# Three of the four lo parts of each MLP pair of a hybrid diffusion step: an accumulating DMA in place of a GpSimd subtraction

## The chip, the cores and the metric

The kernel runs on one core of a Trainium2 chip. The metric is the time of one execution in device microseconds (us), as the median of several executions. Five engines work side by side, each through its own instructions in order: TensorE (PE, matmuls; PEld is its weight load), VectorE (DVE), ScalarE (ACT), GpSimd (POOL) and SyncE (SP, which here only issues DMAs). An instruction waits at the head of its engine's queue until the semaphores that it needs have been raised, and everything behind it on that engine waits with it.

## What is computed

One layer of a diffusion backbone over 128 context and 1024 latent tokens: a token mixer (differential attention and a convolution branch), then a gated MLP with a depthwise convolution of width 3. The part that matters here is the first half of the MLP (`D_MODEL` = 1024, `D_FF` = 2816):

```python
h = rmsnorm(x, lp['w_norm2']) * (1.0 + scale2) + shift2
up = dwconv(h @ lp['w_up'], lp['w_ffn_dw'])
ff = (jax.nn.silu(up[..., :D_FF]) * up[..., D_FF:]) @ lp['w_down']
x = x + gate2 * ff
```

## The kernel before

All weights and activations are float32. A matmul is made of three: every operand is split into a hi part, which is the value rounded to the type float32r, and a lo part, which is the value less its hi part, and the product is hi·hi + hi·lo + lo·hi. So each block of weights needs two tiles, `whi` and `wlo`, ahead of its first use. `prep_to` makes them, in the order of the list `SEQ`: a cast on ACT writes `whi` (L180), and a subtraction `raw - whi` writes `wlo` (L182), on DVE for the first two blocks and on POOL for all others.

The tokens stand in three groups of 384 columns. `w_up` is worked through in 22 pairs of blocks of 128 columns (one of the left half, one of the right half of `up`). Pair 0 is done plainly. Pairs 1 to 21 (`pair(i)`) treat the first two token groups with seven products instead of eight (sums of quarters of the weights against sums of quarters of the activations), and the third group plainly. For this each pair needs four operand sets of 128 x 1024, `w{i}_0` to `w{i}_3`, called w0 to w3 here: w0 and w3 lie in buffers of the tag `raw`, w1 and w2 in buffers of the tag `rawx`, two buffers of each. `fetch_pair` loads them with three DMAs on SP: L155 (all of w3's buffer, 512 KB), L156 (half of w0's) and L157 (half of w2's), 256 KB each; the other halves are sums that DVE makes (L164), called just ahead of the cast in `prep_to`. A buffer is loaded again once the cast and the subtraction that read it are done.

One pair is 11 units of 12 matmuls (L1487): seven products (`prod`) and four quarters of the third token group (`third`). Each set is used in two products and one or two of those quarters. Its successor is prepared inside the same pair: w0 after the products that use it (`prep(5)` behind `p6`), w1 behind `p7`, w2 behind `c2`, w3 at the end. `whi` and `wlo` have one buffer for each place in the ring of four, so a cast waits until PE's last matmul with that set is done.

PE writes into PSUM banks named `f`, `T`, `O` and `S`; ACT (L1566, L1596, L1603) and DVE (L1563) take the results out and free the banks. The depthwise convolution of a pair's two halves follows on ACT (L1477, the first tap; L1618, silu) and DVE (L1479, taps two and three, two for each half; L1620, the product of the halves), and SP stores the result to `scr_fscr` (L1538). In the first pairs DVE also works off a list of small dot products in the background (L1194). After the pairs comes the second half of the MLP (`down`), where POOL already issues accumulating DMAs of 384 KB (L1683, tile `hx`).

The order of the instructions on each engine isn't written out: the program's scheduler sets it from its own timeline, when the kernel is built.

Of the kernel before, what the change touches and what calls it, by code (L numbers as in the profile page):

```python
# [8 lines left out]
F32 = mybir.dt.float32  # L9
F32R = mybir.dt.float32r  # L10
AF = mybir.ActivationFunctionType
ALU = mybir.AluOpType
# [86 lines left out]
SEQ = ORDER + FILL + TAIL + MERGE + WO + WO + FFN  # L99
# [10 lines left out]
class Kernel:  # L110
# [59 lines left out]
    def prep_to(self, p):  # L170
        nc = self.nc
        while self.prepped < min(p, len(SEQ)):
            self.fetch_to(self.prepped + 1)
            raw, make = self.raw.pop(0)
            pool = next(self.wring)
            hi, lo = (pool.tile([128, 1024], F32R, tag=t, name=t, bufs=3 if pool is self.wp else 1)
                      for t in ("whi", "wlo"))
            if make:
                make()
            nc.scalar.copy(hi, raw)  # L180
            eng = nc.vector if self.prepped < 2 else nc.gpsimd
            eng.tensor_tensor(out=lo, in0=raw, in1=hi.bitcast(F32), op=ALU.subtract)  # L182
            self.w[self.prepped] = (SEQ[self.prepped], hi, lo)
            self.prepped += 1
        self.fetch_to(self.prepped + self.fetch_ahead)

    def take(self, name, ahead=2):
        p = self.pos
        assert SEQ[p] == name, (SEQ[p], name)
        self.prep_to(p + 1)  # L190
        self.pos += 1
        got = self.w.pop(p)
        self.late_prep = p + 1 + ahead
        return got[1], got[2]
# [1713 lines left out]
```

## Time and profile before

| what | us |
|---|---|
| median of 3 runs | 1810.08 (1808.92 to 1811.53) |
| the profiled execution, whole | 1811.61 |
| the profiled execution, span from first to last instruction | 1809.8 |
| PE busy | 1690.3 (93% of the span) |
| DVE busy | 1253.8 (69%) |
| ACT busy | 691.0 (38%) |
| POOL busy | 819.0 (45%), of which the two groups of L182: 325.7 and 107.2 |

Busy time is summed over the span. PE is the engine with the least idle time, but the table doesn't tell what ends its waits in one stage. For that the views by stretch and by wait are needed. The stretch of the program in which the change works is about 1040 to 1500 us from the span's start.

### The profile page before, as it was taken

Reading aid. Unit: us, or ns where it says so; the run is one execution under the profiler, and the core shown is the slowest. Engines: PE = TensorE matmul, PEld = TensorE weight load, DVE = VectorE, ACT = ScalarE, POOL = GpSimd, SP = SyncE. Lnnn points to the kernel's source line nnn. Section 1 sums busy time; section 2 is a strip of 40 time slices with the busy share of each in tenths; the row PEclk is TensorE's granted clock in tenths of the full one; section 3 lists DMA queues with packets and bytes.
Section 4 is the critical chain, followed back from the end, with each engine's and each line's share of the span. In section 5 each row is a group of like instructions: output and inputs, shape, how many; then the busy total and the mean of one; then the engine's idle time right before and its main releaser. Section 6 shows DMA issues by size and latency. Waiting matters only on the chain.

```text
span 1809.8 us, 25328 instructions
## 1 busy us (share of the span) xinstructions
PE 1690.3 (93%) x9928; PEld 1649.2 (91%) x9928; DVE 1253.8 (69%) x1594; ACT 691.0 (38%) x1106; POOL 819.0 (45%) x507
## 2 busy tenths in 40 slices
PE   5999889989989999899998999999999999999997
PEld 3889889988989999888998999899999999999997
DVE  5868994698796663697679787878677675333335
ACT  4424454445544553311226533333334336211111
POOL 2545782683873422544343443534434447533311
PEclk8999999999999999999999999999999999999999
DMA  8264223424325424665842222222222226623102
GB/s 307 89 187 142 95 83 100 143 74 136 100 77 177 153 85 134 233 226 179 289 160 85 84 80 70 89 69 80 85 79 73 73 81 194 186 99 99 62 13 105
DMA packets 102446, 220.49 MB, mean 122 GB/s; under 512 B 10004, under 2 KB 60856, under 8 KB 100280
## 3 DMA queue, kind: packets, MB, share of 16 engines
q1 hardware_dynamic: 45264, 120.15, 19.6%
q10 hardware_dynamic: 51592, 79.08, 13.8%
q0 software_dynamic: 5472, 19.66, 3.7%
q8 instruction: 78, 1.28, 0.3%
q14 instruction: 40, 0.33, 0.1%
HBM read 161.55 MB, written 57.30 MB: 121 GB/s over the span
## 4 chain that ended last, share of the span: by engine, by line
PE 45%; DVE 22%; issue 9%; DMA 5%; ACT 4%; POOL 4%; ACTq 0%; POOLq 0%; SPq 0%; DVEq 0%
PE f L230 14%; PE T L230 7%; DVE conv L639 5%; PE S L1487 5%; PE T L1487 4%; PE f L1487 4%; PE O L230 3%; PE O L1487 2%; DVE X L1479 2%; DVE mx L781 2%; DMA tg<-scr_gscr 2%; PE O L822 2%; DVE S L1194 2%; DVE e L794 2%; POOL wlo L182 1%
## 5 line engine op out<-in xcount | busy, mean ns | idle before, releaser
L182 POOL TENSOR_TENSOR wlo<-raw,whi 128x1024 fp32r<-128x1024 f32 x124 | 325.7, 2627 | 468.8 <-ACT whi L180 445.6
L230 PE MATMUL f<-h1h,whi 128*128 128x384 f32 x680 | 233.7, 346 | 4.1 <-ACT gt L602 3.3
L230 PE MATMUL f<-h1l,whi 128*128 128x384 f32 x680 | 234.6, 345 | 0.0
L230 PE MATMUL f<-h1h,wlo 128*128 128x384 f32 x680 | 232.3, 342 | 0.0
L180 ACT CAST whi<-raw 128x1024 fp32r<-128x1024 f32 x126 | 131.9, 1047 | 233.8 <-PE f L230 49.4
L1479 DVE SCALAR_TENSOR_TENSOR X<-X,vec,X 128x1153 f32<-128x1153 f32 x88 | 159.1, 1812 | 75.8 <-ACT X L1477 75.2
L639 DVE SCALAR_TENSOR_TENSOR conv<-glu,vec,conv 128x967 f32<-128x967 f32 x120 | 199.3, 1661 | 1.1
L182 POOL TENSOR_TENSOR wlo<-rawx,whi 128x1024 fp32r<-128x1024 f32 x42 | 107.2, 2558 | 104.7 <-ACT whi L180 97.4
L652 POOL TENSOR_TENSOR conv<-conv,tap 128x200 f32<-128x200 f32 x120 | 115.3, 961 | 68.5 <-ACT tap L646 66.0
L230 PEld LDWEIGHTS f<-h1h,whi 128*128 128x128 f32 x680 | 130.3, 192 | 5.8 <-ACT gt L602 4.0
L230 PEld LDWEIGHTS f<-h1l,whi 128*128 128x128 f32 x680 | 130.9, 192 | 0.4
L230 PEld LDWEIGHTS f<-h1h,wlo 128*128 128x128 f32 x680 | 130.2, 192 | 0.2
L781 DVE TENSOR_REDUCE mx<-S 128x1 f32<-128x1152 f32 (+1 forms) x72 | 88.7, 1231 | 32.0 <-PE S L775 32.0
L783 ACT ACTIVATE e<-S,mx 128x1152 f32<-128x1152 f32 (+1 forms) x72 | 81.2, 1128 | 68.4 <-DVE mx L781 57.0
L646 ACT ACTIVATE tap<-glu,vec 128x200 f32<-128x200 f32 x120 | 55.5, 462 | 106.6 <-POOL conv L652 90.6
L230 PE MATMUL T<-ff,whi 128*128 128x384 f32 x360 | 92.2, 335 | 1.5 <-ACT hx L1679 1.5
L230 PE MATMUL f<-ff,whi 128*128 128x384 f32 x340 | 87.1, 335 | 0.6 <-ACT hx L1679 0.6
L180 ACT CAST whi<-rawx 128x1024 fp32r<-128x1024 f32 x42 | 43.8, 1049 | 110.0 <-DVE rawx L164 74.2
L774 PE MATMUL S<-K,q 128*128 128x384 f32 (+1 forms) x200 | 69.3, 347 | 13.4 <-ACT e L783 13.4
L811 DVE TENSOR_TENSOR atl<-T,ath 128x512 fp32r<-128x512 f32 (+1 forms) x100 | 52.0, 538 | 31.5 <-ACT ath L810 31.2
L1239 DVE SCALAR_TENSOR_TENSOR hx<-f,g,hx 128x128 f32<-128x128 f32 (+1 forms) x64 | 31.6, 515 | 58.8 <-PE f L230 58.7
L1239 DVE SCALAR_TENSOR_TENSOR hx<-T,g,hx 128x256 f32<-128x256 f32 (+1 forms) x66 | 32.4, 512 | 54.3 <-PE T L230 54.0
(435 smaller groups left out, 4947.1 us busy)
## 6 DMA issues: line engine op xcount, KB each, us to landing
raw<-in_wst SPq DMA_DIRECT2D x105, 512.0 KB, 4.0
X<-scr_fscr POOLq DMA_DIRECT2D x20, 576.0 KB, 5.0
scr_fscr<-X SPq DMA_DIRECT2D x22, 512.0 KB, 3.0
scr_gscr<-gate ACTq DMA_DIRECT2D x48, 192.0 KB, 2.0
tg<-scr_gscr SPq DMA_DIRECT2D x24, 384.0 KB, 4.2
ada<-in_ada SPq DMA_DIRECT2D x8, 1024.0 KB, 9.8
araw<-in_ada ACTq DMA_DIRECT2D x16, 512.0 KB, 4.1
K<-scr_kscr ACTq DMA_DIRECT2D x4, 1920.0 KB, 8.2
```

Source lines behind the costliest of these rows:

```text
L180: nc.scalar.copy(hi, raw)
L182: eng.tensor_tensor(out=lo, in0=raw, in1=hi.bitcast(F32), op=ALU.subtract)
L230: nc.tensor.matmul(out, lhsT=a, rhs=b, start=(i == 0), stop=(i == n - 1))
L639: t = nc.vector.scalar_tensor_tensor(out=o, in0=glu[:, j:j + CSPLIT], scalar=w[:, j:j + 1], in1=o, op0=ALU.mult, op1=ALU.add)
L646: nc.scalar.activation(out=p, in_=glu[:, CSPLIT + j:CONVW + j], func=AF.Copy, scale=w[:, j:j + 1])
L652: t = nc.gpsimd.tensor_tensor(out=o, in0=o, in1=p, op=ALU.add)
L774: nc.tensor.matmul(S[:, j, :cw], lhsT=qt[:, c, o:o + 128], rhs=self.K[:, c, ks], start=True, stop=False)
L781: nc.vector.tensor_reduce(out=mx[:, 1:2], in_=src, axis=AX.XY, op=ALU.min)
L783: nc.scalar.activation(out=e[:, :w].rearrange("p (a b) -> p a b", a=nk), in_=src, func=AF.Exp, scale=-1.0, bias=mx[:, 1:2], accum_out=self ...
L1239: nc.vector.scalar_tensor_tensor(out=d, in0=ps[:, o:o + ln], scalar=gate[:, j, c:c + 1], in1=d, op0=ALU.mult, op1=ALU.add)
L1479: nc.vector.scalar_tensor_tensor(out=y[:, :L], in0=u[:, t:t + L], scalar=w[:, t:t + 1], in1=y[:, :L], op0=ALU.mult, op1=ALU.add)
L1487: nc.tensor.matmul(ps[:, :CH], lhsT=a[:, ws], rhs=b[:, k], start=first and k == 0 and i == 0, stop=last and k == 3 and i == 2)
```

## The change

For the sets w0, w1 and w2 of pairs 2 to 21 (60 of the 84 sets) the subtraction on POOL goes. In its place ACT writes minus the hi part into `wlo` (a copy with scale -1, behind the cast), and a DMA on POOL's queue adds the raw values to it, from one place in SBUF to another. Set w3 of every pair, and all of pair 1, keep the subtraction.

```diff
             nc.scalar.copy(hi, raw)
-            eng = nc.vector if self.prepped < 2 else nc.gpsimd
-            eng.tensor_tensor(out=lo, in0=raw, in1=hi.bitcast(F32), op=ALU.subtract)
+            if self.by_dma(SEQ[self.prepped]):
+
+                nc.scalar.activation(out=lo, in_=hi.bitcast(F32), func=AF.Copy, scale=-1.0)
+                nc.gpsimd.dma_start(out=lo.bitcast(F32), in_=raw, accum_op=ALU.add)
+            else:
+                eng = nc.vector if self.prepped < 2 else nc.gpsimd
+                eng.tensor_tensor(out=lo, in0=raw, in1=hi.bitcast(F32), op=ALU.subtract)
...
+    def by_dma(self, name):
+
+        if name[0] != "w" or name[1] == "o":
+            return False
+        i, u = map(int, name[1:].split("_"))
+        return i > 1 and u < 3
```

Lines below this place move down by 12 (L1487 is L1499 after the change); L182 becomes L187 where it stays, the negating copy is L183 and the DMA L184.

The scheduler orders the other engines anew. Three places show it. The first is ACT at the preparation of pair 5's sets; `whi_9817`, `whi_9852` and `whi_9890` are w0, w1 and w2 of pair 5. Before:

```order
L1566 COPY acc_9759<-S_6703 128x384
L1477 ACTIVATE X1_9148<-X0_9141,vec_67 128x1153
L180 CAST whi_9817<-raw_9753 128x1024
L180 CAST whi_9852<-rawx_9755 128x1024
L180 CAST whi_9890<-rawx_9754 128x1024
L1596 COPY X0_9141<-S_6703 128x384
L1477 ACTIVATE X1_9148<-X0_9141,vec_67 128x1153
```

The same place after the change, where `whi_9826`, `whi_9862` and `whi_9901` are those sets:

```order
L1578 COPY acc_9768<-S_6703 128x384
L1189 DMA X2_9366<-in_ada2 128x1024
L180 CAST whi_9826<-raw_9762 128x1024
L183 ACTIVATE wlo_9827<-whi_9826 128x1024
L180 CAST whi_9862<-rawx_9764 128x1024
L183 ACTIVATE wlo_9863<-whi_9862 128x1024
L180 CAST whi_9901<-rawx_9763 128x1024
L1608 COPY X0_9141<-S_6703 128x384
L183 ACTIVATE wlo_9902<-whi_9901 128x1024
L1489 ACTIVATE X1_9148<-X0_9141,vec_67 128x1153
```

Each cast has a negating copy behind it, and the copy for w2 stands ahead of the next first tap (L1477, now L1489).

The second place is POOL at the same sets, before:

```order
L182 TENSOR_TENSOR wlo_9818<-raw_9753,whi_9817 128x1024
L182 TENSOR_TENSOR wlo_9853<-rawx_9755,whi_9852 128x1024
L182 TENSOR_TENSOR wlo_9891<-rawx_9754,whi_9890 128x1024
L182 TENSOR_TENSOR wlo_9940<-raw_9752,whi_9939 128x1024
L182 TENSOR_TENSOR wlo_10012<-raw_9944,whi_10011 128x1024
```

POOL there after the change:

```order
L184 DMA wlo_9827<-raw_9762 128x1024
L184 DMA wlo_9863<-rawx_9764 128x1024
L184 DMA wlo_9902<-rawx_9763 128x1024
L187 TENSOR_TENSOR wlo_9952<-raw_9761,whi_9951 128x1024
L184 DMA wlo_10024<-raw_9956 128x1024
```

Three of four subtractions are DMA issues now, and the one for w3 stays in its place.

The third place is PE where pair 5 begins; `whi_9817` and `wlo_9818` are w0 of pair 5, the first row is the last matmul with a set of pair 4 ahead of it. Before:

```order
L1487 MATMUL S_6703<-h2h_8906,wlo_9698 128x384
L1487 MATMUL f_9953<-hx_8657,whi_9817 128x384 x2
L1487 MATMUL f_9953<-hx_8657,wlo_9818 128x384
L1487 MATMUL f_9953<-hx_8657,whi_9817 128x384 x2
L1487 MATMUL f_9953<-hx_8657,wlo_9818 128x384
```

PE there after the change, where `whi_9826` and `wlo_9827` are w0 of pair 5 and `whi_9862` is w1:

```order
L1499 MATMUL S_6703<-h2h_8906,wlo_9706 128x384
L1499 MATMUL f_9965<-hx_8657,whi_9826 128x384 x2
L1499 MATMUL T_9979<-h2h_8906,whi_9826 128x384
L1499 MATMUL T_9979<-h2l_8907,whi_9826 128x384
L1499 MATMUL O_9992<-hx_8658,whi_9826 128x384 x2
L1499 MATMUL f_10007<-hx_8659,whi_9862 128x384 x2
L1499 MATMUL T_10029<-op_8660,whi_9862 128x384 x2
L1499 MATMUL f_9965<-hx_8657,wlo_9827 128x384
```

Ten matmuls with hi parts, from five chains, now stand ahead of the first one with the lo part, where there were two. Between the last matmul with w0 of pair 4 and this one stand 51 matmuls; before, 50.

## Rows read from the trace of the kernel before

**Rows 1.** Windows: busy time by engine, 1040 to 1500 us (engine, busy us, instructions).
```profile
1040.00:1500.00 460.00, 443.19 (x2511) 440.70 (x2511) 350.36 (x407) 170.80 (x193) 201.46 (x77) 0.99 0.24 79
```
**Rows 2.** Waits of PE, 1040 to 1500 us (us in total, times, longest).
```profile
PE S L1487 <- DVE acc L1563: 6.6, 3, 2.9
PE S L1487 <- DVE X L1563: 5.5, 2, 3.0
PE f L1487 <- DVE X L1563: 3.2, 1, 3.2
PE f L1487 <- POOL wlo L182: 1.0, 1, 1.0
```
**Rows 3.** One line's or tile's instructions, 1055 to 1500 us (ns minimum/median/maximum).
```profile
L1479 DVE SCALAR_TENSOR_TENSOR X<-X,vec,X x76: 1408/1422/3575, 1055.6 to 1497.0; 128x1153 f32<-128x1153 f32 x76
...
L164 DVE TENSOR_TENSOR raw<-raw x18: 677/680/2887, 1066.9 to 1471.5; 128x512 f32<-128x512 f32 x18
```
**Rows 4.** Timeline of DVE ahead of PE's wait at 1143.9 (start us, us).
```profile
1136.70 2.85 DVE L164 TENSOR_TENSOR raw<-raw 128x512 f32<-128x512 f32 x1
...
1140.81 3.50 DVE L164 TENSOR_TENSOR rawx<-raw 128x512 f32<-128x512 f32 x2
...
1146.16 0.54 DVE L1563 TENSOR_TENSOR acc<-S,acc 128x384 f32<-128x384 f32 x1
```
**Rows 5.** Timeline of POOL beside it.
```profile
1135.52 3.49 POOL L182 TENSOR_TENSOR wlo<-rawx,whi 128x1024 fp32r<-128x1024 f32 x1
1140.77 2.39 POOL L182 TENSOR_TENSOR wlo<-raw,whi 128x1024 fp32r<-128x1024 f32 x1 [1.76 <-ACT whi L180]
```
**Rows 6.** Timeline of DVE and POOL ahead of PE's wait at 1219.
```profile
1216.42 3.54 DVE L1620 TENSOR_TENSOR X<-X 128x1153 f32<-128x1153 f32 x1
...
1215.88 2.87 POOL L182 TENSOR_TENSOR wlo<-raw,whi 128x1024 fp32r<-128x1024 f32 x1 [3.74 <-ACT whi L180]
```
**Rows 7.** Windows of PE with the granted clock (busy us, matmuls, clock).
```profile
1054.50:1057.90 3.40, 3.40 (x13) 0.51 0.69 253
```
**Rows 8.** Chain that ended last: a run of matmuls without a gap.
```profile
711.71 8.33 PE T L230 x48
```
**Rows 9.** Timeline of DVE and POOL, 1529.5 to 1533 us, where POOL issues DMAs.
```profile
1529.60 1.41 DVE L1479 SCALAR_TENSOR_TENSOR X<-X,vec,X 128x1153 f32<-128x1153 f32 x1
1531.11 1.36 DVE L1620 TENSOR_TENSOR X<-X 128x1153 f32<-128x1153 f32 x1
...
1530.51 1.77 POOL L1683 DMA_DIRECT2D hx<-scr_xscr  x2
```
**Rows 10.** Lines by form, ACT, 1040 to 1500 us (busy us, mean ns, idle before).
```profile
L1477 ACT ACTIVATE X<-X,vec 128x1153 f32<-128x1153 f32 x39 | 49.0, 1261 | 7.2 <-DMA scr_fscr<-X 4.5 <-DVE X L1563 2.1
L180 ACT CAST whi<-raw 128x1024 fp32r<-128x1024 f32 x39 | 40.9, 1049 | 99.7 <-PE S L1487 39.4 <-DMA raw<-in_wst 31.9 <-DVE raw L164 16.8
```
**Rows 11.** Waits of DVE, 1040 to 1500 us.
```profile
DVE X L1479 <- ACT X L1477: 62.5, 29, 5.6
```
**Rows 12.** Tile hx, 1510 to 1640 us: the accumulating DMAs of 384 KB.
```profile
L1683 POOL DMA_DIRECT2D hx<-scr_xscr x12: 848/1232/1866, 1521.0 to 1545.8; - x12
...
DMA to landing us min/median/max: 5.8/9.2/16.6
```
**Rows 13.** DMA queues, 1555.5 to 1557.8 us: accumulating packets alone (packets, MB, share).
```profile
q0 software_dynamic: 176, 0.49, 109.8%
```
**Rows 14.** DMA issues of the page (KB each, median us to landing).
```profile
X<-scr_fscr POOLq DMA_DIRECT2D x20, 576.0 KB, 5.0
```
**Rows 15.** Timeline of ACT: the cast of w0 of pair 5.
```profile
1091.44 1.06 ACT L180 CAST whi<-raw 128x1024 fp32r<-128x1024 f32 x1 [4.25 <-PE S L1487]
```
**Rows 16.** Waits of the DMA queue of SP, 1040 to 1500 us.
```profile
SPq L156 <- POOL wlo L182: 188.6, 18, 18.0
...
SPq L157 <- POOL wlo L182: 48.6, 18, 4.1
```

## The prediction, made before the changed kernel ran

> **What bounds the kernel now.** I read the busy times of the stretch first, then what PE waits for there, then what the engine it waits for was doing. The change lies between 1040 and 1500 us. There PE is busy for 443 of 460 us and runs at 0.99 of its clock, so at most some 17 us of idle time and a little clock can be won; POOL is busy for only 201 us, so its own load isn't the limit [rows 1]. Nearly all of PE's idle time is six waits for DVE, to free a PSUM bank: 6.6 + 5.5 + 3.2 = 15.3 us. One wait of 1.0 us is for a `wlo` from POOL [rows 2]. DVE, at 350 of 460 us, isn't full either; it comes late at six places.
>
> Why it comes late is seen by setting the two timelines side by side. The first of L164's additions takes 0.68 us at its median and up to 2.89, the tap of L1479 1.42 and up to 3.58: two kinds of run, not a spread [rows 3]. At 1136.70 the addition starts 1.2 us after a POOL subtraction of 3.49 us has begun and ends just after it; at 1140.81 two more take 3.50 us beside the next subtraction [rows 4, 5]. So a DVE instruction that reads two SBUF tensors stands still while POOL subtracts. In that row of work DVE lost 2.85 - 0.68 = 2.2 us and 3.50 - 2 x 0.68 = 2.1 us, and the bank was read out at 1146.16, when PE had stood for 2.9 us [rows 2, 4]. Ahead of the wait at 1219, L1620 takes 3.54 us beside a subtraction [rows 6], against 1.36 us without one [rows 9], again 2.2 us lost. The other four waits show one or the other picture.
>
> **What the change removes.** 60 of the 77 subtractions in this stretch go, some 60 x 2.6 us of POOL time that nobody waits for, and with them the hold on DVE. The question is whether the DMA issue that takes their place holds DVE as well. Where POOL issued accumulating DMAs for 1.77 us without a pause, L1479 took 1.41 us and L1620 1.36 us, their undisturbed times [rows 9]. So I take the issue as free for DVE; the other end, that it holds DVE for its own 0.85 to 1.87 us [rows 12], is a rival below. What comes back at the six waits: the two of the L1620 picture (5.5 us together) get 2.2 us each, since the subtraction for w3 a little earlier stays: 4.4 us. The other four (6.6 + 3.2 = 9.8 us) have two holds of 2.1 or 2.2 us ahead of them, more than each wait is long, so I take all: 9.8 us. Sum 14.2 us.
>
> PE's clock adds to it. After four of these waits PE shows 3.4 us at the lower level, 0.5 of 2.4 GHz: 13 matmuls in the 3.4 us [rows 7], some of them counted at the edges, where the undisturbed step of 8.33 / 48 = 0.174 us [rows 8] would give 19.6. At half the clock a stretch of 3.4 us loses at most 1.7 us, and 6.6 x 0.174 = 1.1 us by the count; I take 1.4 x 4 = 5.6 us, gone with the waits. The gain is 14.2 + 5.6, about 20 us.
>
> **What it adds on ACT.** 60 negating copies of 128 x 1024. L1477 takes 1.26 us for 1153 columns, the cast 1.05 us for 1024 [rows 10], so 1.05 to 1.12 us each, 67 us at most. ACT has the room, 171 of 460 us [rows 1]. Those who stand behind a copy in ACT's queue are the first tap L1477, for which DVE already waits 62.5 us in 29 waits [rows 11], and the copies out of PSUM, for which PE waits. The order shows the copy for w2 ahead of the next first tap. A delay of 1.1 us hits PE only where DVE is then late for a bank again: nothing at the low end, 1.1 us at each of the six places at the high end, 6.6 us. I take half, 3 us, because the DVE work ahead of these places is 2 to 4 us shorter than now.
>
> **What it adds as latency.** A lo part was ready 2.4 to 3.5 us after its cast [rows 5]. Now it is the copy, the issue and the landing. No row shows a transfer of 512 KB from SBUF onto SBUF. The nearest are the accumulating DMAs of 384 KB: 5.8 us at the least, which is the one that found the queue nearly empty, 9.2 at the median and 16.6 at the most, where up to six stood in the queue [rows 12]. Size: in a stretch that holds only such packets, 176 packets (18 of them of 4 bytes) fill 16 engines for 2.3 us, so 16 x 2.3 x 1.098 / 158 = 0.256 us for one of 3072 bytes, or 0.34 us for 4096 [rows 13]; with 8 packets on each engine (128 rows over 16) 512 KB take 8 x (0.34 - 0.256) = 0.7 us longer. A plain load of 576 KB on the same queue lands in 5.0 us [rows 14]. So the low end is 5.0, the high end 16.6; I take 5.8 + 0.7 = 6.5, near the low end, since between 1040 and 1500 us the DMA engines are busy for 0.24 of the time [rows 1].
>
> The tightest place is w0 of pairs 5, 9, 12, 16 and 19. Its cast starts when PE has done the last matmul with the old w0 [rows 15], and in the new order 51 matmuls stand between that one and the first that reads the new lo part: 51 x 0.174 = 8.9 us. Needed are 1.05 + 1.1 + 6.5 = 8.65, and some 0.2 us of hand-over: 8.85 us. It just fits, with nothing to spare. w2 in pairs 6, 13 and 20 has 61 to 63 matmuls (10.6 to 10.9 us), with two more ACT instructions ahead of its copy, and just fits as well. w0 of pairs 8 and 15 has 62; all others have 69 or more, 12 us. So every microsecond that the landing takes beyond 6.5 costs up to 8 us. At 5.8 nothing is lost; I take 0.3 us on average, 2 us.
>
> The Trainium skill (DMA: Bandwidth & Descriptors, Anatomy of one DMA — SWDGE (gpsimd) path) gives 2.0 us and the bytes over 436 GB/s for a DMA from POOL, by which 512 KB would take 3.2 us, and these 2 us would be nought; the trace speaks against it for this kind, with 5.8 us for 384 KB at the least [rows 12].
>
> Last, the loads. A buffer is free only when the DMA that reads it has landed, some 6 us later than now. SP waits at L157 for w1's lo part, 48.6 us in 18 waits (2.7 us each), and the issue of L156 stands behind it, which itself waits 188.6 us in 18 waits (10.5 us each) for the subtraction of w3 [rows 16]. That stays, and covers the 6 us on average: nothing.
>
> Sum: 1809.8 - 20 + 3 + 2 = 1794.8 us of span. The profiled execution took 1811.6 us with a span of 1809.8, and lay 1.5 above the median of 1810.1; so the median should be 0.3 us above the span, **1795 us**.
>
> **Rivals.** First, the ACT copies give half of it back: the delays come to 6.6 us and two of the six waits stay with their clock (5 us more): 1795 + 3.6 + 5 = 1804 us. For it speaks that DVE already waits for L1477; against it that DVE's lost time is larger than the copies.
>
> Second, the lo parts land late, the one that ends on the other side. With 9 us the eight tight places lose 8 x 2.5 = 20 us less the 2 counted, 1813 us, and this is the point from which it decides. With 10 us they lose 28, the two places with 62 matmuls join with 2 x 1.5, and five lower-clock stretches add 7: 1795 - 2 + 38 = 1831 us. For it speak the median of 9.2 us and that some transfers share the queue with the loads, or that w1's and w2's casts follow closely; against it that the 9.2 belongs to a full queue.
>
> A second way to be late is at the start: that POOL can't write a DMA's descriptors while DVE runs. If each issue had to wait out one L1479, 1.4 us [rows 3], the eight places would lose 8 x 1.4 = 11 us more, 1806 us. Against it: the issues beside L1479 and L1620 stayed at 0.9 us each [rows 9], and these two lines are the bulk of DVE's work in the stretch. The Trainium skill (SBUF — State Buffer, SBUF: two separate sides) has it as a rule that DVE in a mode that uses both its ports keeps GpSimd from writing descriptors; no row here shows a DVE instruction that does so.
>
> Third, the change doesn't do what it says for DVE: the issue holds it for 1.2 us in place of 2.1. Then 0.9 of each 2.1 us comes back, 20 x 0.43 = 9 us, less 5: 1806 us. Rows 9 speak against it.
>
> **How the numbers follow.** The forecast has 0.52, the ACT rival 0.18, the late landing 0.18 (0.06 near 9 us, which ends as no change, 0.12 beyond), the late start 0.04, the hold by the issue 0.08. A run of this kernel can tell about 0.2%, 3.6 us, from no change. The last two end at the bound of 1806 and count half as faster, half as the same. Faster: 0.52 + 0.16 + 0.02 + 0.04 = 0.74; same: 0.02 + 0.06 + 0.02 + 0.04 = 0.14; slower: 0.12. The range reaches from 1788 us (all of the 20 us, nothing added, 1790, and some small waits more) to 1814 us, the point at which the late landing decides; 0.12 lie above and some 0.07 below.
>
> **What would show it.** Right: L1479, L1620 and L164 at their short times in nearly every run but beside w3's subtraction; PE's waits for DVE between 1040 and 1500 us at 3 us or less in place of 15; the accumulating DMAs landing in 6 to 7 us, and no waits of PE for a DMA into `wlo`. Wrong: PE waiting for that DMA at the beginning of pairs 5, 9, 12, 16 and 19, or DVE's long runs still there.

## The result, and the profile after

The changed kernel takes **1790.28 us** (median of 4 runs, 1788.7 to 1791.63), beside 1810.8 us for the kernel before on the same chip: a ratio of 0.9886 (0.9873 to 0.9898). The forecast was 1795 us, the range 1788 to 1814 us. The profiled execution has a span of 1788.3 us in place of 1809.8.

Where the 21.5 us of span went can be told from three points of the trace. The first matmul of the 22 pairs starts at 965.6 us in place of 968.4; that is ahead of the change's place, and over all the kernels of this study this point lies between 964.0 and 969.6 us (once, where the stage ahead was edited, at 980.9), so it isn't the change's. From that matmul to the last of the pairs, 2916 of them, it takes 532.7 us in place of 551.3: 18.7 us less. What follows takes 290.0 us in place of 290.2. This middle part is called the pair stage below.

Busy time by engine, 1040 to 1500 us of the kernel after (PE, PEld, DVE, ACT, POOL, each with its instructions; granted clock, DMA share, GB/s), which answers to [rows 1]:

```profile
1040.00:1500.00 460.00, 454.55 (x2604) 452.46 (x2603) 291.96 (x416) 237.72 (x265) 113.55 (x85) 1.00 0.61 152
```

PE is busy for 11 us more, DVE for 58 us less with the same work and more of it done, ACT for 67 us more, POOL for 88 us less, and the DMA share is 0.61 in place of 0.24. Waits of PE in the same stretch, all that are listed (us in total, times, longest), for [rows 2]:

```profile
PE S L1499 <- DVE X L1575: 3.3, 1, 3.3
PE O L1499 <- DMA wlo<-raw: 0.7, 1, 0.7
PE S L1499 <- DVE acc L1575: 0.6, 1, 0.6
PE S L1499 <- DMA wlo<-rawx: 0.5, 1, 0.5
PE S L1499 <- ACT X L1608: 0.3, 1, 0.3
```

The six waits for DVE, 15.3 us, have become two of 3.9 us. A seventh of 0.5 us, which [rows 2] don't show, is gone, and so is the wait for POOL; 1.2 us of waits for the new DMAs have come. The instructions of single lines on DVE, 1055 to 1500 us (ns minimum/median/maximum), for [rows 3]:

```profile
L1491 DVE SCALAR_TENSOR_TENSOR X<-X,vec,X x75: 1408/1422/3039, 1057.6 to 1498.5; 128x1153 f32<-128x1153 f32 x75
...
L164 DVE TENSOR_TENSOR raw<-raw x18: 677/680/694, 1059.5 to 1451.8; 128x512 f32<-128x512 f32 x18
...
L1632 DVE TENSOR_TENSOR X<-X x19: 1347/1352/3581, 1062.7 to 1477.2; 128x1153 f32<-128x1153 f32 x19
```

L164 has lost its long runs altogether; of L1632 one run is still long. The timeline of DVE and POOL of the kernel after at the place of [rows 6] (start us, us):

```profile
1199.47 2.50 DVE L1491 SCALAR_TENSOR_TENSOR X<-X,vec,X 128x1153 f32<-128x1153 f32 x1 [1.47 <-ACT X L1489]
...
1205.04 1.35 DVE L1632 TENSOR_TENSOR X<-X 128x1153 f32<-128x1153 f32 x1
...
1198.37 2.39 POOL L187 TENSOR_TENSOR wlo<-raw,whi 128x1024 fp32r<-128x1024 f32 x1 [3.05 <-ACT whi L180]
1206.03 0.87 POOL L184 DMA_DIRECT2D wlo<-raw  x1 [5.27 <-ACT wlo L183]
```

w3's subtraction at 1198.37 still holds a tap, 2.50 us in place of 1.42. The product at 1205.04, which [rows 6] show with 3.54 us, has an issue beside it and takes 1.35 us. Over the stage, 13 of the L1632 products have more than 0.3 us of an issue beside them, and their mean is 1.351 us; the five with nothing on POOL beside them have 1.354 us. For each DVE instruction from 1040 to 1480 us, take its time above the shortest run of the same line, operation and shape in the same trace. Added up, that is 81 us in the kernel before and 19 us in the one after. That sum is called held time below.

### The profile page after: what moved, and what is told of

Same layout as the page of the kernel before. It is cut to its first block, busy times and chain, and to the rows that moved or that the text cites. A ratio compares the mean times of both kernels' runs of the same rounds, so it can differ in the third digit from the quotient of the medians.

```text
span 1788.3 us, 25510 instructions
## 1 busy us (share of the span) xinstructions
PE 1682.3 (94%) x9928; PEld 1644.2 (92%) x9928; DVE 1177.2 (66%) x1594; ACT 751.1 (42%) x1166; POOL 713.3 (40%) x507
## 3 DMA queue, kind: packets, MB, share of 16 engines
q0 software_dynamic: 14112, 51.12, 13.4%
## 4 chain that ended last, share of the span: by engine, by line
PE 52%; DVE 18%; DMA 8%; issue 8%; POOL 5%; ACT 3%; ACTq 1%; POOLq 0%; DVEq 0%; SPq 0%
PE f L242 15%; PE T L242 7%; DVE conv L651 7%; PE S L1499 6%; PE f L1499 6%; PE T L1499 6%; PE O L242 3%; PE O L1499 3%; DVE mx L793 2%; DMA tg<-scr_gscr 2%; PE O L834 2%; DVE e L806 2%; POOL wlo L187 1%; DVE S L1206 1%; DMA hx<-in_ada 1%
## 5 line engine op out<-in xcount | busy, mean ns | idle before, releaser
L187 POOL TENSOR_TENSOR wlo<-raw,whi 128x1024 fp32r<-128x1024 f32 x104 | 270.2, 2599 | 389.0 <-ACT whi L180 370.8
L180 ACT CAST whi<-raw 128x1024 fp32r<-128x1024 f32 x126 | 132.0, 1048 | 243.7 <-DMA raw<-in_wst 59.4
L1491 DVE SCALAR_TENSOR_TENSOR X<-X,vec,X 128x1153 f32<-128x1153 f32 x88 | 139.7, 1593 | 91.6 <-ACT X L1489 91.0
L184 POOL DMA_DIRECT2D wlo<-rawx x40 | 34.4, 860 | 141.6 <-ACT wlo L183 122.9
L180 ACT CAST whi<-rawx 128x1024 fp32r<-128x1024 f32 x42 | 44.0, 1047 | 62.0 <-PE S L1499 23.7
```

Of the source, the lines that this page charges most:

```text
L1491: nc.vector.scalar_tensor_tensor(out=y[:, :L], in0=u[:, t:t + L], scalar=w[:, t:t + 1], in1=y[:, :L], op0=ALU.mult, op1=ALU.add)
```

## The experiments

Three theories were to be told apart: that DVE is held by POOL's subtractions at places where a PSUM bank is due (the prediction's), that it is the sum of DVE's time that counts, and that the gain hangs on the DMA itself. Beside these stand the prices of lateness and of ACT's copies, which the prediction had taken without a row that shows them. All 12 kernels and the one after:

| kernel | median us | ratio to before | pair stage us | held time us |
|---|---|---|---|---|
| before | 1809.4 to 1810.8 | 1 | 551.3 | 81 |
| after | 1790.28 | 0.9886 (0.9873 to 0.9898) | 532.7 | 19 |
| e1, copy on ACT, sum on POOL | 1803.01 | 0.9957 (0.9941 to 0.9973) | 543.7 | 76 |
| e2, w3 by DMA too | 1820.77 | 1.0054 (1.0035 to 1.0074) | 561.0 | 4 |
| e3, two DMAs for each set | 1903.76 | 1.0519 (1.0492 to 1.0547) | 644.2 | 16 |
| e4, w0 alone by DMA | 1788.55 | 0.9883 (0.986 to 0.9906) | 531.9 | 42 |
| e5, w0 alone, on DVE | 1797.08 | 0.9925 (0.9897 to 0.9952) | 537.0 | 52 |
| e6, w1 and w2 alone by DMA | 1796.04 | 0.9916 (0.9892 to 0.994) | 537.7 | 48 |
| e7, e4 with two DMAs in a chain | 1813.72 | 1.0018 (1.0002 to 1.0033) | 560.6 | 52 |
| e8, e4 and the mixer's blocks | 1802.74 | 0.9952 (0.9939 to 0.9965) | 530.2 | 41 |
| e9, after with each copy made twice | 1802.42 | 0.9955 (0.9938 to 0.9971) | 544.6 | 18 |
| e10, e4 with each copy made three times | 1786.34 | 0.9875 (0.985 to 0.9899) | 528.5 | 41 |
| e11, w0, w1, w2 on DVE, no DMA | 1783.78 | 0.9857 (0.9831 to 0.9883) | 525.0 | 26 |
| e12, e11 and the mixer's blocks | 1785.85 | 0.9854 (0.9834 to 0.9874) | 524.6 | 25 |

Each ratio is to runs of the kernel before on the same chip. The pair stage is from the one profiled execution of each kernel. The scheduler sets a new order for each kernel, so the difference between two kernels is that of the edit and of the new order together; where that changes a reading, it is said.

**e1: the copy stays, the sum goes back to POOL.**

```diff
                 nc.scalar.activation(out=lo, in_=hi.bitcast(F32), func=AF.Copy, scale=-1.0)
-                nc.gpsimd.dma_start(out=lo.bitcast(F32), in_=raw, accum_op=ALU.add)
+                nc.gpsimd.tensor_tensor(out=lo, in0=raw, in1=lo.bitcast(F32), op=ALU.add)
```

> The 60 lo parts are made of the same negating copy on ACT, but POOL adds the raw values with a tensor_tensor in place of the DMA. If the gain is DVE's release from POOL's subtractions, the holds come back: L1491 (two taps) at a mean of 1.75 us or more in the stretch of the pairs instead of 1.54, PE's waits for DVE there at 12 us or more, and the time at 1808 to 1816 us, some us above the kernel before by what the ACT copies cost. If the gain came from the new order on PE, DVE and ACT or from the earlier splitting of the work, it stays near 1790 to 1796 us.

Measured: 1803.01 us, faster than expected by 5 us at the least. DVE is held nearly as before (76 us), but the copy puts POOL's work for w0 1.1 us later, and at some places that is enough to let a DVE instruction pass. Timeline of DVE and POOL of e1, at the place of [rows 6]:

```profile
1208.45 1.35 DVE L1632 TENSOR_TENSOR X<-X 128x1153 f32<-128x1153 f32 x1
...
1209.08 3.60 POOL L184 TENSOR_TENSOR wlo<-raw,wlo 128x1024 fp32r<-128x1024 f32 x1 [4.90 <-ACT wlo L183]
```

In the kernel before, the subtraction began 0.54 us ahead of the product, which then took 3.54 us; here the product is first, takes 1.35 us, and POOL is the one that is long. The wait at 1219 us is gone and so is the one at 1387. Five waits for DVE to free a bank remain, as the waits of PE from 1000 to 1500 us show:

```profile
PE S L1499 <- DVE acc L1575: 8.7, 3, 3.9
PE T L1499 <- DVE acc L1575: 1.4, 1, 1.4
...
PE f L1499 <- DVE X L1575: 1.1, 1, 1.1
```

So over a third of the gain is had with no work taken from POOL and little less held time in sum: the place of a hold counts.

**e4 and e6: one part of the change alone.**

```diff
-        return i > 1 and u < 3
+        return i > 1 and u == 0
```

e6 has `u in (1, 2)` there.

> Only w0 of pairs 2 to 21 goes by the DMA, 20 of the 60 sets. In the trace of the kernel before, w0's subtraction was one of the holds ahead of every wait of PE for DVE that was looked at. If the gain hangs on the holds at those places, w0 alone brings more than its third: 10 to 14 us, 1797 to 1801 us. If it goes by POOL's or DVE's time in sum, it brings a third, 7 us, about 1804 us.

> Only w1 and w2 by the accumulating DMA; w0 and w3 by GpSimd's subtraction. If the holds by w0 are the whole cause, the waits of PE for DVE stay at 10 us or more and the time is 1800 to 1808 us. If each set has its share of the gain by the time that GpSimd no longer spends, two thirds of the gain come: 1796 us or less.

Measured: e4 has the whole gain with a third of the DMAs and more than twice the held time, and is faster than both of its expectations. e6 has about three quarters of the gain; that refutes w0 as the whole cause, and taken alone it lies at the edge of a share by set (1796 us). Together the two speak against shares, since the 20 sets and the other 40, added up, give far more than all 60. Waits of PE in e4, 1040 to 1500 us, all over 0.4 us:

```profile
PE f L1499 <- DVE X L1575: 3.2, 1, 3.2
PE O L1499 <- DMA wlo<-raw: 0.5, 1, 0.5
```

and in e6, 1000 to 1500 us, the waits for DVE:

```profile
PE S L1499 <- DVE acc L1575: 3.1, 2, 2.1
...
PE f L1499 <- DVE X L1575: 1.1, 1, 1.1
...
PE T L1499 <- DVE acc L1575: 1.0, 1, 1.0
PE S L1499 <- DVE X L1575: 0.7, 1, 0.7
```

In [rows 4, 5] DVE is held twice ahead of one bank: once by a subtraction with an operand of the tag `rawx` (w1 or w2), then by that of w0. Each hold is 2.1 or 2.2 us and the wait that follows 2.9 us, so with either of them gone the rest of the wait should be under 1 us. e4 has no wait at that place; e6 has waits of 0.7 to 2.1 us for DVE, and 3.3 us for lo parts that land late. A wait that needs two holds goes for the most part with either of them, and so the two parts of the change don't add up.

The one long wait that e4 keeps, 3.2 us at 1043, has a hold by a set that still goes by POOL ahead of it (DVE and POOL of e4):

```profile
1042.40 2.85 DVE L1206 CUSTOM_DVE_ANT_0 X<-X,mod 128x512 f32<-128x512 f32 x1
...
1042.00 2.69 POOL L187 TENSOR_TENSOR wlo<-rawx,whi 128x1024 fp32r<-128x1024 f32 x1 [2.92 <-ACT whi L180]
```

That instruction takes 0.74 us without a subtraction beside it.

**e5 and e11: the subtraction on DVE itself.**

```diff
-            eng = nc.vector if self.prepped < 2 else nc.gpsimd
+            eng = nc.vector if self.prepped < 2 or self.by_dma(SEQ[self.prepped]) else nc.gpsimd
             eng.tensor_tensor(out=lo, in0=raw, in1=hi.bitcast(F32), op=ALU.subtract)
```

This is against the kernel before. e5 has only w0 in `by_dma`, e11 has w0, w1 and w2; neither has a copy on ACT or a DMA.

> The w0 subtraction of each pair from the third on is made on DVE; w1, w2 and w3 stay on GpSimd, as in the kernel before. There is no DMA into a lo part and no copy on ACT. If the hold that GpSimd's w0 subtraction puts on DVE, just ahead of a bank that PE waits for, is the cause: DVE pays about 20 x 1.2 us of its own time, but at a known place, and the holds of 2.1 to 2.2 us go, so 1788 to 1798 us, and PE's waits for DVE between 1040 and 1500 us fall to some 5 us. If the gain needs the DMA or the ACT copy (because they shift the w0 part later in the order), DVE's own subtraction lies where the hold lay and the time stays at 1804 us or more.

> All 60 subtractions of w0, w1 and w2 on DVE, none by DMA, no copies on ACT; w3 stays on GpSimd. Nothing holds DVE but w3, and DVE pays 60 x 1.2 us = 72 us itself. If the holds were the whole cost of the kernel before and DVE's sum does not matter (283 us of 440 are used in the changed kernel): 1790 to 1798 us, as with w0 alone on DVE (1797.1 us). If each microsecond on DVE ahead of a bank release counts as a hold does (1.2 us in place of 2.1), the waits come back with more than half their length: 1800 to 1812 us.

Measured: e5 is within the hold theory's range, near its upper end, with 7.3 us of waits for DVE in place of the 5 us expected. e11 is under both theories, with the lowest median of all kernels. In e5, DVE and POOL ahead of a wait of 5.0 us at 1235:

```profile
1229.90 3.42 DVE L182 TENSOR_TENSOR wlo<-raw,whi 128x1024 fp32r<-128x1024 f32 x1
...
1234.58 2.83 DVE L1201 CUSTOM_DVE_ANT_0 X<-X,mod 128x512 f32<-128x512 f32 x1
...
1229.39 2.85 POOL L182 TENSOR_TENSOR wlo<-rawx,whi 128x1024 fp32r<-128x1024 f32 x1 [7.28 <-ACT whi L180]
1234.20 2.66 POOL L182 TENSOR_TENSOR wlo<-rawx,whi 128x1024 fp32r<-128x1024 f32 x1 [1.96 <-ACT whi L180]
```

DVE's own subtraction, 1.22 us when nothing is beside it, is held to 3.42 us by POOL's for another set, and 4.7 us later the next one holds L1201. In e11 w1's and w2's subtractions are gone from POOL too. Busy time in e11, 1040 to 1500 us:

```profile
1040.00:1500.00 460.00, 459.78 (x2652) 459.31 (x2651) 363.43 (x473) 186.36 (x214) 68.39 (x32) 1.00 0.26 89
```

w0's subtractions on DVE cost their own time there and no more (one line's instructions, ns minimum/median/maximum, e11):

```profile
L182 DVE TENSOR_TENSOR wlo<-raw,whi x19: 1207/1218/1222, 1044.9 to 1453.2; 128x1024 fp32r<-128x1024 f32 x19
```

PE is busy for 459.8 of 460 us. DVE is at 363 us, more than in the kernel before, and no wait of PE for it is listed in that stretch. So neither the DMA nor ACT's copy is needed for the gain, and the sum of DVE's time isn't the cause. Whether e11 beats the kernel after is likely rather than shown: their ratios, 0.9857 and 0.9886, are from two sets of runs, and their intervals overlap from 0.9873 to 0.9883. The pair stage is 7.6 us shorter.

**e2 and e3: more by DMA, and later.** e2 takes w3 as well:

```diff
-        return i > 1 and u < 3
+        return i > 1
```

e3 copies minus two times the hi part and adds the raw values twice:

```diff
-                nc.scalar.activation(out=lo, in_=hi.bitcast(F32), func=AF.Copy, scale=-1.0)
+                nc.scalar.activation(out=lo, in_=hi.bitcast(F32), func=AF.Copy, scale=-2.0)
+                nc.gpsimd.dma_start(out=lo.bitcast(F32), in_=raw, accum_op=ALU.add)
                 nc.gpsimd.dma_start(out=lo.bitcast(F32), in_=raw, accum_op=ALU.add)
```

> The fourth set (w3) of pairs 2 to 21 goes by the DMA as well, so no POOL subtraction is left beside DVE's work in pairs 3 to 20. If DVE's hold is the cause, L1491 falls to 1.42 us in nearly every run and the last wait of PE for DVE there goes: 2 to 5 us less than the changed kernel, 1786 to 1789 us, if the lo part of w3 isn't late. If it is late (in three pairs PE needed it 6.4 us after the old set's last use, where cast, copy and a landing of 4.5 to 5.6 us take 7 to 8), 3 to 6 us come back and it ends at 1789 to 1793 us.

> ACT writes minus twice the hi part, and two accumulating DMAs, one after the other, add the raw values twice: the lo part comes out doubled, so the result isn't the reference's. This puts about 5 us on every lo part's way. By the prediction's price (eight tight places, up to 8 us for each us beyond what fits) it costs 15 to 35 us, 1805 to 1825 us, less what a new order of PE's work hides. If the landing is hidden anyway, it stays within 3 us of the changed kernel, 1787 to 1794 us.

Both came out far slower than expected. In e2 the held time is down to 4 us, and the kernel is slower than before. Waits of PE in e2, 1000 to 1500 us, the first two and the first of DVE:

```profile
PE f L1499 <- DMA wlo<-raw: 8.7, 7, 3.7
PE O L1499 <- DMA wlo<-raw: 2.9, 3, 1.5
PE f L1499 <- DVE X L1575: 2.3, 1, 2.3
```

and waits of DVE in e2, 1040 to 1500 us:

```profile
DVE raw L164 <- DMA wlo<-raw: 30.7, 16, 4.2
```

In the kernel after, L164 waits at three places, 9.1 us, for w3's subtraction. With w3 by DMA it waits at 16, since it writes into a buffer of the tag `raw` that an accumulating DMA has yet to read to its end; the wait stands at the head of DVE's queue. The loads into these buffers come later as well, and the casts behind them. The casts of w0 and w3 on ACT, 1040 to 1500 us (idle before, and for what), in the kernel after and in e2:

```profile
L180 ACT CAST whi<-raw 128x1024 fp32r<-128x1024 f32 x42 | 44.2, 1052 | 112.4 <-DMA raw<-in_wst 47.3 <-PE S L1499 44.3 <-issue 8.9
...
L180 ACT CAST whi<-raw 128x1024 fp32r<-128x1024 f32 x38 | 39.9, 1049 | 170.9 <-DMA raw<-in_wst 111.6 <-PE S L1499 31.2 <-DVE X L1575 13.4
```

Of PE's waits for lo parts, 9.8 us are for w0 at seven places, and 2.7 us for w3 itself in pairs 5, 12 and 19, three places as the expectation had it. The edit that looked like more of the same lengthened the chain that was tight. That is read from the waits and not tested apart, and some 7 of the 28 us by which e2's pair stage is longer than the kernel after's are neither in PE's waits nor at a lower clock.

In e3 a second issue waits in POOL's queue for the first to land, and every issue behind it waits too. Waits of PE (1000 to 1500 us) and of POOL (1040 to 1500 us) in e3:

```profile
PE f L1500 <- DMA wlo<-raw: 20.5, 6, 7.8
PE T L1500 <- DMA wlo<-rawx: 14.7, 7, 3.2
...
POOL wlo L185 <- DMA wlo<-rawx: 160.1, 31, 8.7
```

e3 so has two causes, the latency and the blocked queue, and can't price one of them. That is why e7 was made.

**e7 and e10: the price of lateness, with w0 alone.** e7 is e4 with the edit of e3. e10 is e4 with two more copies:

```diff
+                nc.scalar.activation(out=lo, in_=hi.bitcast(F32), func=AF.Copy, scale=-1.0)
+                nc.scalar.activation(out=lo, in_=hi.bitcast(F32), func=AF.Copy, scale=-1.0)
                 nc.scalar.activation(out=lo, in_=hi.bitcast(F32), func=AF.Copy, scale=-1.0)
```

> As the kernel with only w0 by DMA (1788.6 us), but with minus two times the hi part and a second accumulating DMA of the same set behind the first, so that w0's lo part comes one DMA later (it gets twice raw minus twice hi, so the output is not the reference's). The price of lateness that the prediction used: 4 to 5 us more at five places with some 9 us of matmuls ahead, so 15 to 25 us more and some clock, 1805 to 1820 us, with PE's waits for the DMA at the beginning of pairs 5, 9, 12, 16 and 19 and nowhere else. If the latency is hidden by more than the count of matmuls says: below 1795 us.

> Only w0 by DMA, with the negating copy made three times, so that the lo part comes 2.1 us later than in the kernel with only w0 by DMA (1788.6 us), where a second DMA in the chain, 4.8 us, cost 25 us. If the price is a step set by the 51 matmuls (8.9 us) at five places: copy, hand-overs and a landing of 4.8 us need 7.1 us, 1.8 us are free, and 2.1 us more cost 5 x 0.3 us: 1788 to 1792 us. If it is in proportion to the latency, 25 x 2.1 / 4.8 = 11 us: 1799 us.

Measured: e7 25 us over e4, within the expectation; e10 1.7 us under its first range, no dearer than e4. That doesn't show a step at a fixed count of matmuls, since the scheduler moved PE's work too. Counted in the traces from the start of w0's cast to PE's first matmul with the new lo part, e4 has 38 to 51 matmuls at its seven tightest places, and e10 has 52 to 57 at the same seven. In e4 the lo part lands there between 0.5 us after PE comes to it and 1.6 us before it, so 2.1 us more would have been too late at all seven in e4's own order. So what e10 adds is hidden at least in part by its new order. One of the places of e7 in the timeline of PE:

```profile
1299.85 0.51 PE L1500 MATMUL f<-op,whi 128*128 128x384 f32 x2
1303.98 0.69 PE L1500 MATMUL O<-hx,wlo 128*128 128x384 f32 x1 [3.63 <-DMA wlo<-raw]
1304.47 0.84 PE L1500 MATMUL O<-hx,whi 128*128 128x384 f32 x2
```

The copy starts at 1293.04, the first DMA lands at 1299.13, the second at 1303.94, and PE goes on 0.04 us later, at a lower clock for a while: two matmuls with hi parts take 0.84 us in place of 0.51. The clock granted over 1040 to 1480 us is 0.97 here and 1.00 in e4. Of the 28.6 us by which e7's pair stage is longer than e4's, 16.3 are PE's waits; the rest goes with the lower clock, which takes 37.5 us of the stage in place of 10.2. One expectation failed: PE waits for this DMA at seven places (18.8 us), not at five, at w0 of pairs 2, 6, 10, 12, 13, 15 and 20. Only pair 12 is among the five named.

**e9: the price of the copies on ACT.** The kernel after, with one more copy of that kind for each set, so one `+` line of the diff of e10.

> The changed kernel with each negating copy made twice, one behind the other, so 60 more ACT instructions of 1.06 us (64 us more on ACT between the third pair and the last) and 1.06 us more until a lo part is ready. If the copies cost time by standing ahead of L1489, L1630 and the copies out of PSUM, as the prediction's 3 us for 60 of them have it, 3 us more or, at its high end, 6.6 us: 1793 to 1797 us. If ACT's room and DVE's slack hide them: within 1 us of 1790.3 us, since the landing at its median (5.6 us) leaves 1 us at the tight places.

Measured: 1802.42 us, 12 us over the kernel after and beyond both expectations. Waits of PE in e9, 1000 to 1500 us:

```profile
PE f L1500 <- DMA wlo<-raw: 6.2, 2, 3.5
PE f L1500 <- DMA wlo<-rawx: 3.0, 3, 1.8
PE T L1500 <- DMA wlo<-rawx: 1.7, 1, 1.7
```

ACT is busy for 282 of 460 us there, and PE waits 1.7 us for ACT or DVE. The rest of its waits, 11 us, is for lo parts. So the copies cost little by standing in ACT's queue; what costs is that lo parts come late. Part of that is the new order. The two longest waits, 3.5 and 2.7 us, are for w0 of pairs 3 and 12, where e9 has 40 and 48 matmuls from the start of the cast to PE's first matmul with the lo part, and landings of 7.1 and 7.0 us. In the kernel after, pair 3 has 61 there, and its lo part is 8.7 us early. So the 12 us aren't the price of 1.06 us alone.

**e8 and e12: the same edits for the stage before.** e8 is e4, and e12 is e11, with the q, k, g, ua, ub and v blocks of the mixer as well, in `by_dma`:

```diff
         if name[0] != "w" or name[1] == "o":
-            return False
+            return name[0] in "qkguv" and self.prepped >= 6
```

> w0 of the MLP pairs by DMA, and also the q, k, g, ua, ub and v blocks of the stage before the MLP, whose subtractions on GpSimd lie beside DVE's two-input work there. If that stage too is held at DVE (PE waits some 35 us for DVE there), 10 to 25 us come off: 1765 to 1780 us. If the blocks are consumed as soon as they come, the landing costs more than the hold: 1795 us or more.

> As the kernel with all 60 on DVE (1783.8 us), and the subtractions of the q, k, g, ua, ub and v blocks of the stage before the MLP on DVE too: about 30 of 1.2 us, 36 us more of DVE's own time there. Between 80 and 960 us DVE loses some 100 us to holds in the kernel before (54 us in its convolution taps alone), and PE waits some 30 us for DVE. If what freed the MLP stage holds here as well, 5 to 20 us come off: 1764 to 1779 us. If DVE is late there because of its own chains (softmax, then the transposed parts), and PE waits for ACT and for those chains, its 36 us come on top at the places where PE waits already: 1784 to 1800 us.

Measured: e8 14 us over e4; e12 no different from e11. The mixer isn't bound that way. Waits of PE in e12, 50 to 980 us:

```profile
PE T L814 <- DVE e L801: 14.8, 6, 6.0
PE S L781 <- ACT e L790: 12.9, 14, 1.9
...
PE T L814 <- DVE atl L818: 3.6, 5, 1.5
```

Held time there, between 80 and 960 us, is 98 us in place of 124 in e11, but PE waits for the softmax chain, which alternates between ACT and DVE (in e11 6.5, 13.4 and 5.7 us in the same three rows), and DVE's added subtractions stand in that chain. In e8 it is the transposed parts that come late (12.6 and 9.1 us).

## Why the prediction was right, step by step

- **What bounds the stage: right.** DVE late at a few banks, held by POOL's subtractions. e4, e5 and e11 show it from three sides: without the subtraction nearest to the bank, with DVE doing it, and with all of them on DVE. Of the signs that were to show it, each came near and none to the letter: waits for DVE of 3.9 us (3 or less), landings of 5.5 us at the median (6 to 7), two waits for a DMA into `wlo`, 1.2 us (none).
- **Removed waits, 14.2 us taken: the size is near, the list was not.** Measured 15.3 - 3.9 = 11.4 us in the stretch, the seventh of 0.5 us, the wait of 1.0 us for POOL, and one of 1.5 us at 1027 us, ahead of the stretch, where L1170 had been held to 3.19 us (1.23 us without). The step that failed is "the other four have two holds ahead of them, I take all": the wait of 3.2 us at 1050 is there again as one of 3.3 us at 1043, from another cause (below). The two of the L1620 picture, for which 1.1 us was kept back, went wholly, though w3's subtraction still holds a tap ahead of the one looked at (2.50 us at 1199.47); e1 shows the same there. Why that hold no longer counts wasn't pursued. So that the sum comes within 1 us of 14.2 is luck in part: it counts one long wait that stayed, and leaves out three short ones and 1.1 us that went.
- **The clock, 5.6 us taken: about 4.** After four waits of the kernel before PE shows a lower clock [rows 7], after only one of the kernel after. Windows of PE there (busy us and matmuls first, clock third from the end):

```profile
1046.50:1050.50 4.00, 3.80 (x13) 3.80 (x14) 1.64 (x4) 2.08 (x4) 0.85 (x1) 0.60 0.95 271
```

  Three stretches less, at the 1.4 us each of the prediction, are 4.2 us. This follows from its own price; no run set the clock apart.
- **The issue of a DMA doesn't hold DVE: right**, by the 13 products at 1.351 us beside issues. This rules out the rival by which the issue holds DVE. The one of a late start has nothing for it either: all 60 issues of the kernel after take 0.85 to 0.92 us. The Trainium skill (SBUF — State Buffer, Who interferes with whom) lets a DVE instruction with two SBUF inputs contend with a GpSimd instruction that reads SBUF; the trace agrees, 3.54 us beside the subtraction and 1.35 us beside the issue.
- **ACT's copies, 3 us taken: too much.** They are 57 in the stretch at 1.058 us, as taken, and PE waits 0.3 us for ACT. Lines by form on ACT of the kernel after (busy us, mean ns, idle before):

```profile
L183 ACT ACTIVATE wlo<-whi 128x1024 fp32r<-128x1024 f32 x57 | 60.1, 1058 | 1.1
L1489 ACT ACTIVATE X<-X,vec 128x1153 f32<-128x1153 f32 x39 | 49.1, 1259 | 12.8 <-DMA scr_fscr<-X 12.2
```

  DVE waits longer for the first tap (82.5 us in 29 waits in place of 62.5), but PE's waits for DVE fell all the same.
- **Latency, 2 us taken: 1.2 us, near in size; the places were others.** Tile `wlo` of the kernel after, from issue to landing, 1040 to 1500 us:

```profile
DMA to landing us min/median/max: 4.5/5.5/9.8
```

  The median is 1 us under the 6.5 us taken (w0's alone 4.8, w1's and w2's 6.0), and the tail reaches the 9 us at which the late rival would decide. "It just fits, with nothing to spare" holds: w0's lo part lands less than 1 us before PE comes to it in pairs 6, 12, 15 and 19 (0.8, 0.1, 0.4 and 0.9 us), and 0.7 us after in pair 13, the longest of these waits. Of these only 12 and 19 are among the five pairs named. The step that failed is "its cast starts when PE has done the last matmul with the old w0": in pair 13 the cast waits another 4.2 us for its load, and 36 matmuls are left from its start, where the list has 69 or more. In the L180 line of the kernel after (at e2), the load ends more of these casts' idle time than PE does, 47.3 and 44.3 us (before, 31.9 and 39.4 [rows 10]). "Up to 8 us per us" stays untested: e7, e9 and e10 each have an order of their own.

  The Trainium skill (DMA: Bandwidth & Descriptors, Anatomy of one DMA — SWDGE (gpsimd) path) would give an estimate of 3.2 us for these 512 KB; the shortest of them takes 4.5 us.
- **The loads at nothing: nearly right in sum, but they were not the whole of it.** SP waits now (waits of SP's DMA queue, 1040 to 1500 us), for [rows 16]:

```profile
SPq L156 <- POOL wlo L187: 107.3, 16, 15.4
SPq L157 <- DMA wlo<-rawx: 93.5, 18, 8.1
SPq L155 <- DMA wlo<-raw: 56.9, 17, 6.2
```

  w3's subtraction still covers L156, as said; e2 shows what it costs when that cover goes. Not foreseen was that other transfers get slower. The longest piece of the chain that ended last in the pair stage of the kernel after, and the DVE instruction that waited for it (start us, us):

```profile
1025.42 9.16 DMA X<-in_ada
...
1034.60 0.75 DVE L1206 CUSTOM_DVE_ANT_0 X<-X,vec 128x512 f32<-128x512 f32 x1 [5.07 <-DMA X<-in_ada]
```

  In the kernel before this load took 3.7 us to the same place, with DVE waiting 0.3 us for it; here two accumulating DMAs are issued beside it, 1.9 us before and 1.5 us after. DVE stands for 5.1 us at a small background product, with the taps queued behind, and the 3.3 us wait of PE at 1043 follows. In e11, with no such DMAs, the load takes 4.1 us and DVE waits 0.7 us, and there is no wait of PE. e2 repeats it: 9.0 us, DVE waits 4.9 us, and PE 2.3 us at 1047. But the accumulating DMAs alone don't do it: e6 has two of them too, 2.6 us before and 1.5 us after, and its load takes 4.7 us. There the weight load L155 was issued 4.8 us ahead, in the kernel after and in e2 0.8 and 0.9 us. So the link from traffic to the wait is read at one place, not proven.

Sum: 11.4 + 0.5 + 1.0 + 1.5 + 4.2 - 1.2 - 0.3 = 17.1 us, less 0.5 for a wait for DVE at the start of the stage (L1336, now L1348) that grew from 0.9 to 1.4 us: 16.6 of the 18.7 us by which the pair stage is shorter. The other 2.1 us are not assigned. The forecast of 1795 us was 5 us too slow. In spans it was 6.5 us (1794.8 and 1788.3): 2.7 us by an earlier start of the stage, which isn't the change's, and 3.7 us because the stage is shorter by 18.7 us where 15 were forecast, most of it the 3 us for the copies. The median came out 2.0 us above the profiled span and not 0.3, so its error is 1.7 us smaller than the span's.

## What to carry to other kernels

Look for two durations of one instruction, and set the other engine's timeline beside them; then ask which of the holds stands ahead of something due. Here taking away w0's 20 subtractions gave the whole gain and taking away the other 40 three quarters of it, since two holds that share one wait don't add up; so try the smallest part of the change alone. Where a scheduler sets the order, compare the orders before a difference is called the price of the edit. Before work goes to a transfer with 5 us of latency, try it on the engine that was held: 1.22 us at a known place was cheaper than 2.1 us at an unlucky one, though DVE's busy time rose.

## What the runs showed of the hardware that was not expected

- An accumulating DMA of 512 KB from SBUF onto SBUF lands in 4.5 us at the least, 4.8 us at the median with w0 alone and 5.5 us with all three sets, whose tail reaches some 10 us; there w0's still have 4.8 us and w1's and w2's 6.0. Plain loads beside 60 of them were slower too: those of 512 KB for `raw` have a median of 5.2 us in place of 4.0.
- A subtraction of 128 x 1024 takes 2.4 us on POOL alone and 1.22 us on DVE alone; side by side with the other engine's two-input work, whichever starts second is the longer by the time that it has to stand: DVE's went to 3.42 us, POOL's to 3.60 us.
- The length of PE's wait alone doesn't tell whether a stretch at the lower clock (0.5 of 2.4 GHz) follows. In the kernel before a wait of 1.8 us ending at 1317.1 was followed by 3.4 us of it and one of 2.4 us ending at 1390.4 by none. In e2 only the longest wait between 1040 and 1480 us, 3.7 us, was followed by it, and the mean clock there is 1.00; in e7 the mean is 0.97.
